# Moving one block product ahead, copies before splits, and two product orders in a two-layer decoder trunk

## The chip, the cores and the metric

The kernel runs on one core of one Trainium2 chip. The metric is device time in microseconds (us); lower is better.

## The reference

Two decoder layers on 512 tokens with 1024 features, all in 32-bit floats. Layer 0 mixes with sliding-window attention and a short convolution, layer 1 with chunked gated linear attention. Each layer then has a gated feed-forward part with a convolution and a per-layer embedding:

```python
for i in range(DEPTH):
    h = _rms_norm(x, mix_norm[i])
    x = x + mixer(h)                       # layer 0: attention and convolution; layer 1: gated linear attention
    x = x + _conv_ffn(_rms_norm(x, ffn_norm[i]), ffn_w_up[i], ffn_conv_w[i], ffn_conv_b[i], ffn_w_down[i])
    x = x + _per_layer_embedding(x, p[i], ple_norm[i], ple_w_gate[i], ple_w_proj[i])

def _conv_ffn(h, w_up, conv_w, conv_b, w_down):
    u = _causal_depthwise_conv(h @ w_up, conv_w) + conv_b
    gate, up = jnp.split(u, 2, axis=-1)
    return (jax.nn.gelu(gate, approximate=False) * up) @ w_down

def _per_layer_embedding(x, p_i, norm, w_gate, w_proj):
    gate = jax.nn.sigmoid(_rms_norm(x, norm) @ w_gate)
    return gate * (p_i @ w_proj)
```

The gate of the linear attention comes from 16 low-rank columns: `log_a = log_sigmoid(g_lr @ w_gate_up + gate_bias) / 16`.

## The kernel before

**Split products.** Every 32-bit operand is cut into a high part (ScalarE, an activation that rounds to `fp32r`) and a low part (VectorE, the operand minus its high part). One product is then three matmuls: high by high, high by low, low by high (`mm3`, L171 to L173). Weights arrive in `raw` (two buffers) by SyncE's DMA queue and are cut by `cut` (L151, L152) or `cut_blocks` (L843, L844) into `wh` and `wl` (three buffers each). Activations are cut by `split` (L109, L110, or L113, L114 with a gain).

**Seven block products.** Some matrix products are taken as 2 x 2 blocks with seven products instead of eight. `seven` (L888) is a generator that issues them on TensorE, 12 matmuls of 256 columns each (L906 to L908). In order: the first goes into bank `W`, and ScalarE copies it into the left halves of `X` and `Y` (L912, L913, by the helper at L900); then it yields. The second goes into `V`, which is copied aside (`so`), the third onto `X` left, the fourth onto `Y` left; `Y` left is copied to `X` right; it yields. Then the last weights are cut, the fifth goes onto `X` right, and `X` right is copied to `Y` right; it yields. The sixth goes onto `Y` left, the seventh onto `X` right, and the last yield gives `X`, `Y` and the copy of `V`. The four forms of the weights are differences of blocks: `first_forms` (L867, L868) and `more_forms` (L875, L878), formed in `raw` by VectorE. `W`, `V`, the projections, transposes and the spread norm share the four PSUM banks of tag `pa`; `X`, `Y` and plain products share the four of tag `ps`.

**Order.** Inside a `manual_schedule` block TensorE runs in the order in which the program is written. The other engines, and TensorE outside such blocks, are put in order by a planner ahead of time: it simulates the kernel with estimated durations and takes, among what is ready on an engine, the one written first; `high_priority` moves work ahead, and `issue_after(ins)` makes what is written in its block come after `ins` on the same engine. A buffer or bank is given out when its first instruction is planned. Each engine then runs its own fixed list.

**Down-projection** (`down`, L1169). A list of plain product parts (`steps`) with block groups between them: four groups in layer 0, three in layer 1. In a group, six matmuls of 512 columns of plain work stand between the block products. `pump` cuts the weights of later parts.

**Layer 0's last stage** (`ple0`, L1368). Four groups of block products for the gate, two feature blocks each; `proj(m)` is the projection of feature block m (six matmuls of 512 columns into a `pa` bank), and `close` applies the norm `R`, the sigmoid (L1417), the projection (L1418) and the residual (L1419). `R` is spread over partitions after group 0 (`spread`, L366, copied by ScalarE at L368). `enter` splits features for layer 1 (L113, L114). Before, per group on TensorE: first product; second to fourth; for groups 1 to 3 a projection; fifth; a projection; sixth and seventh. Group 0's two projections stand ahead of everything.

**Layer 1's mixer** (`mixer1`). `log_decays` turns the low-rank columns (L1735), splits them (L1740 to L1742) and multiplies (L1746), written after the first query product. TensorE is ordered by the planner here. **Layer 1's last stage** (`ple1`, L1457) has its own `proj` over tokens, with `mm3`; its order is written by hand for TensorE, VectorE and ScalarE.

Of the kernel before, what the change touches and what calls it, by code (L numbers as in the profile page):

```python
# [15 lines left out]
ALU = mybir.AluOpType  # L16
# [7 lines left out]
ND = D // P  # L24
# [39 lines left out]
class Kernel:  # L64
# [1104 lines left out]
    def down(self, i, acts, forms, both, work, finish, copied, ahead):  # L1169
# [100 lines left out]
        with tc.manual_schedule(engines={ET.PE}):  # L1270
            with tc.high_priority(offset=300):
                for _ in range(2):
                    load(loads.pop(0))
                with tc.issue_after(copied.ins):
                    pump(0)
            for t, (u, name, k0, k1, s) in enumerate(plan):
                if t in ahead:
                    ahead[t]()
                own = u not in banks
                if own:  # L1280
                    banks[u] = [self.ps(), self.ps()]
                ends = t + 1 == len(plan) or plan[t + 1][0] != u
                joined = i == 0 and u == 3

                def steps(lo, hi):
                    for k in range(lo, hi):
                        for c in range(2):
                            self.mm3(
                                banks[u][c], cuts[t](k, c * P, (c + 1) * P), acts[rows[name][0] + k0 + k],
                                start=own and k == 0, stop=ends and k == k1 - k0 - 1, skip_group_check=joined,  # L1290
                            )

                def settled(ends):
                    nonlocal next_unit
                    if ends:
                        for c in range(2):
                            add(2 * u + c, banks[u][c])
                        due[u] -= 1
                    while not block_left and next_unit < 4 and not due[next_unit]:
                        for m in (2 * next_unit, 2 * next_unit + 1):  # L1300
                            finish(m)
                        next_unit += 1

                if s is None:
                    steps(0, k1 - k0)
                    settled(ends)
                    pump(1)
                    pend()
                    if work:
                        work.pop(0)()  # L1310
                        if not work:
                            load_inner(inner.pop(0))
                else:
                    g = gens[s]
                    steps(0, 1)
                    next(g)
                    steps(1, 2)
                    next(g)
                    steps(2, 3)
                    next(g)  # L1320
                    cut_done(s)
                    pump(1)
                    steps(3, 4)
                    pump(1)
                    settled(ends)
                    X, Y, V = next(g)
                    pump(1)
                    x = self.xT[2 * s + 1].rearrange("p (u t) -> p u t", u=2)
                    nc.vector.tensor_tensor(x, x, V.unsqueeze(1).to_broadcast([P, 2, H]), ALU.add)
# [38 lines left out]
    def ple0(self, fp, both, next_gain):  # L1368
# [17 lines left out]
        def prepare(raw, odd=None, last=None):  # L1386
            ev, od = self.by_parity(raw)
            return self.seven(od, self.seven_forms(ev, od, raw, odd), operands, lambda: result()[:, :H], True, last)

        pT = self.pT  # L1390
        steps = prepare(load(0), self.odd_split, self.last_split)
        wj = self.wj

        def proj(m):
            pj = self.pa()
            c = slice(m * P, (m + 1) * P)
            for k in range(2):
                self.mm3(pj, [w[:, k, c] for w in wj], pT[k], start=k == 0, stop=k == 1)
            return pj

# [21 lines left out]
        late = None  # L1422
        with tc.manual_schedule(engines={ET.PE}):
            pjs = [proj(0), proj(1)]
            for g in range(groups):
                ends = g + 1 == groups
                if not ends:
                    raw = load(g + 1)
                next(steps)
                if late:  # L1430
                    close(*late)
                if ends:
                    enter(0, 1)
                copied = next(steps)
                if ends:
                    enter(2, 3)
                if g:
                    pjs = [proj(2 * g)]
                else:
                    self.end_norm()  # L1440
                    self.begin_norm(None)
                next(steps)
                if g:
                    pjs.append(proj(2 * g + 1))
                last = steps
                if not ends:
                    with nullcontext() if g else tc.issue_after(copied.ins):
                        steps = prepare(raw)
                late = g, next(last), pjs
                if g == 0:  # L1450
                    R = self.spread()
            enter(4, 5)
            close(*late)
            enter(6, 7)
        self.end_norm()

    def ple1(self, fp):  # L1457
# [63 lines left out]

        def proj(t, w):
            pj = self.pa()
            for k in range(2):
                self.mm3(pj, sl(pT[k], t), (w[0][:, k, :], w[1][:, k, :]), start=k == 0, stop=k == 1)
            return pj

        def result():
# [110 lines left out]
    def mixer1(self):  # L1639
# [4 lines left out]
        with tc.tile_pool(name="m1", bufs=1) as mp:  # L1644
# [31 lines left out]
            def pair_w(c0):  # L1676
                return self.weights(w_in[:, :, c0 : c0 + 256], ND, 256)

            def feature(w, c):
                ps = self.ps()  # L1680
                for k in range(ND):
                    self.mm3(ps, w(k, c * P, (c + 1) * P), xg[k], start=k == 0, stop=k == ND - 1)
                return ps

            def query(w, h):
                o = qT[h] = self.fp.tile([P, S], F32, tag="a0", name=self.nm("qT"))
                nc.vector.scalar_tensor_tensor(
                    out=o, in0=feature(w, h % 2), scalar=float(GDK**-0.5), in1=R, op0=ALU.mult, op1=ALU.mult
                )

            def key(w, h):
# [23 lines left out]
            las = []  # L1715

            def gate_up():

# [9 lines left out]
                nc.vector.tensor_tensor(ws[64:96], w[64:96], t[64:96].bitcast(F32), ALU.subtract)  # L1728
                return ws

            def log_decays():

                ps = self.pa()
                for t in range(NT):
                    nc.tensor.transpose(ps[:GR, t * P : (t + 1) * P], glr[:, t, :], self.ident)  # L1735
                gT = self.sp.tile([P, S], F32R, tag="R", name="gT")
                nc.vector.tensor_copy(
                    gT[:96].rearrange("p (a b) -> p a b", b=P), self.ones[:96].unsqueeze(1).to_broadcast([96, NT, P])
                )
                nc.scalar.activation(gT[:GR], ps[:GR], AF.Copy)  # L1740
                nc.scalar.activation(gT[64 : 64 + GR], ps[:GR], AF.Copy)
                nc.vector.tensor_tensor(gT[32 : 32 + GR], ps[:GR], gT[:GR].bitcast(F32), ALU.subtract)  # L1742
                es, pzs = [], []
                for h in range(GH):
                    pz = self.pa()
                    mm(pz, wgs[:96, h * GDK : (h + 1) * GDK], gT[:96], start=True, stop=True)  # L1746
                    e = new()
                    nc.scalar.activation(e, pz, AF.Abs)
                    pzs.append(pz)
                    es.append(e)  # L1750
                for e in es:
                    nc.scalar.activation(e, e, AF.Exp, scale=-1.0)
                for e in es:
                    nc.scalar.activation(e, e, AF.Ln, bias=1.0)
                for h, (e, pz) in enumerate(zip(es, pzs)):
                    la = mp.tile([P, S], F32, tag=f"lah{h}", name=self.nm("la"))
                    nc.vector.scalar_tensor_tensor(
                        out=la, in0=pz, scalar=0.0, in1=e, op0=ALU.min, op1=ALU.subtract
                    )
                    las.append(la)  # L1760
# [346 lines left out]
```

## Time and profile before

| | |
|---|---|
| median of 3 runs | 1200.19 us (1199.80 to 1201.39) |
| the profiled execution | 1199.51 us, its span 1197.5 us |
| granted TensorE clock | 1.00 |
| TensorE matmuls in use | 99% of the span |
| TensorE weight loads | 90% |
| VectorE | 83% |
| ScalarE | 58% |
| GpSimd | 4% |
| HBM traffic | 97 GB/s over the span |

A timeline row is: start in us from the span's start, duration in us, engine, line of the kernel, operation, out<-in, shape, and in brackets the idle time before it and what ended that. PE is TensorE, PEld its weight loads, DVE VectorE, ACT ScalarE, POOL GpSimd. Matmuls are pipelined and the end of one is modelled, so stalls of TensorE are best read from start to start. A row of the waits is: engine and line, what it waited for, total us, how often, the longest. A row of stretches is: stretch, length, then busy us (and instructions) of PE, PEld, DVE, ACT and POOL, the clock, the DMA share and GB/s.

Stages of the span: layer 0's mixer to about 135 us, its feed-forward part to 520, its last stage 521 to 575; layer 1's mixer to about 740, its feed-forward part to 1138, its last stage to the end.

### The profile page before, as it was taken

The page shows a single profiled execution, that of the slowest core. Times are in us where ns is not written, and L with a number is a line of the kernel's source. Part 1 is how long each engine was busy: PE and PEld are TensorE (multiplying, and loading weights), DVE is VectorE, ACT ScalarE, POOL GpSimd, SP SyncE. Part 2 cuts the span into 40 slices and gives each one's busy share as a digit, 9 for nine tenths or more (in the row PEclk, how much of TensorE's full clock was granted, in tenths as well). Part 3 has the DMA queues.
Part 4 walks back from the last instruction along what each step waited for, and adds up shares of the span by engine and source line. Part 5 has one row for each costly group of instructions (what it writes and reads, how often), then busy time and mean ns, then how long its engine had stood idle before and what let it go on. Part 6 is the DMA issues. An engine that isn't in the chain of part 4 may idle for free.

```text
span 1197.5 us, 20218 instructions
## 1 busy us (share of the span) xinstructions
PE 1188.8 (99%) x8218; PEld 1079.3 (90%) x8218; DVE 993.4 (83%) x1593; ACT 690.6 (58%) x1137; POOL 45.2 (4%) x64
## 2 busy tenths in 40 slices
PE   9999999999999999999999999999999999999998
PEld 8877789999999989889978988899999999888887
DVE  6786687898999986899779876687989999978595
ACT  7466565655565653766663655555555556655374
POOL 2610000000000000000100000000000000000000
PEclk9999999999999999999999999999999999999999
DMA  7232222333332342321322222223333333323601
GB/s 223 73 95 81 74 88 71 106 106 106 106 104 91 126 136 86 129 71 61 115 94 71 73 69 71 88 72 111 101 112 101 106 106 115 124 89 97 211 1 71
DMA packets 112928, 117.76 MB, mean 98 GB/s; under 512 B 2840, under 2 KB 107858, under 8 KB 112836
## 3 DMA queue, kind: packets, MB, share of 16 engines
q1 hardware_dynamic: 112000, 115.88, 29.9%
q8 instruction: 64, 1.05, 0.4%
q0 software_dynamic: 560, 0.42, 0.3%
q14 instruction: 28, 0.23, 0.1%
q10 hardware_dynamic: 276, 0.18, 0.1%
HBM read 114.37 MB, written 2.10 MB: 97 GB/s over the span
## 4 chain that ended last, share of the span: by engine, by line
PE 89%; DVE 7%; ACT 2%; issue 1%; DMA 1%; ACTq 0%; POOL 0%; DVEq 0%
PE ps L171 12%; PE ps L172 12%; PE ps L173 12%; PE pa L173 7%; PE pa L172 7%; PE pa L171 7%; PE ps L906 6%; PE ps L908 6%; PE ps L907 5%; PE pa L908 2%; PE pa L906 2%; PE pa L907 2%; PE ps L1505 1%; PE ps L1504 1%; PE ps L1503 1%; DVE wl L152 1%
## 5 line engine op out<-in xcount | busy, mean ns | idle before, releaser
L152 DVE TENSOR_TENSOR wl<-raw,wh 128x1024 fp32r<-128x1024 f32 (+4 forms) x142 | 162.7, 1147 | 41.7 <-ACT wh L151 41.0
L151 ACT ACTIVATE wh<-raw 128x1024 fp32r<-128x1024 f32 (+4 forms) x142 | 141.2, 997 | 83.6 <-PE ps L172 54.0
L843 ACT ACTIVATE wh<-raw 128x1024 fp32r<-128x1024 f32 x90 | 95.6, 1063 | 125.6 <-DVE raw L868 84.2
L961 DVE SCALAR_TENSOR_TENSOR zt<-z,vfa,zt 128x510 f32<-128x510 f32 (+1 forms) x176 | 131.0, 745 | 0.3
L844 DVE TENSOR_TENSOR wl<-raw,wh 128x1024 fp32r<-128x1024 f32 x90 | 110.0, 1222 | 16.5 <-ACT wh L843 15.2
L173 PE MATMUL pa<-b,wl 128*128 128x256 f32 x352 | 97.3, 276 | 0.0
L173 PE MATMUL pa<-a,wl 128*128 128x256 f32 x352 | 97.3, 276 | 0.0
L171 PE MATMUL pa<-b,wh 128*128 128x256 f32 x352 | 97.2, 276 | 0.0
L172 PE MATMUL pa<-b,wh 128*128 128x256 f32 x352 | 97.2, 276 | 0.0
L171 PE MATMUL pa<-a,wh 128*128 128x256 f32 x352 | 97.2, 276 | 0.0
L172 PE MATMUL pa<-a,wh 128*128 128x256 f32 x352 | 97.2, 276 | 0.0
L959 ACT ACTIVATE zt<-z,vfb 128x512 f32<-128x512 f32 x88 | 71.3, 810 | 18.2 <-DVE z L951 9.2
L171 PE MATMUL ps<-b,wh 128*128 128x512 f32 x192 | 76.7, 399 | 0.0
L172 PE MATMUL ps<-b,wh 128*128 128x512 f32 x192 | 75.1, 391 | 0.0
L173 PE MATMUL ps<-b,wl 128*128 128x512 f32 x192 | 75.0, 390 | 0.0
L173 PEld LDWEIGHTS pa<-b,wl 128*128 128x128 f32 x352 | 66.1, 188 | 0.1
L172 PEld LDWEIGHTS pa<-a,wh 128*128 128x128 f32 x352 | 66.1, 188 | 0.0
L172 PEld LDWEIGHTS pa<-b,wh 128*128 128x128 f32 x352 | 66.1, 188 | 0.0
L171 PEld LDWEIGHTS pa<-a,wh 128*128 128x128 f32 x352 | 66.1, 188 | 0.0
L171 PEld LDWEIGHTS pa<-b,wh 128*128 128x128 f32 x352 | 66.1, 188 | 0.0
L173 PEld LDWEIGHTS pa<-a,wl 128*128 128x128 f32 x352 | 66.1, 188 | 0.0
L906 PE MATMUL ps<-four,wh 128*128 128x256 f32 x232 | 64.6, 279 | 0.0
(468 smaller groups left out, 3759.1 us busy)
## 6 DMA issues: line engine op xcount, KB each, us to landing
raw<-in_ffn_w_up_dram SPq DMA_DIRECT2D x42, 1024.0 KB, 4.9
raw<-in_ffn_w_down_dram SPq DMA_DIRECT2D x13, 1024.0 KB, 5.2
raw<-in_hy_w_in_dram SPq DMA_DIRECT2D x8, 1024.0 KB, 5.0
raw<-in_gla_w_in_dram SPq DMA_DIRECT2D x8, 1024.0 KB, 5.1
raw<-in_ffn_w_down_dram SPq DMA_DIRECT2D x8, 768.0 KB, 4.7
raw<-in_ple_w_gate_dram SPq DMA_DIRECT2D x6, 1024.0 KB, 5.2
raw<-in_hy_w_out_dram SPq DMA_DIRECT2D x16, 256.0 KB, 4.2
raw<-in_gla_w_out_dram SPq DMA_DIRECT2D x4, 1024.0 KB, 4.9
```

The source lines that it names most:

```text
L151: nc.scalar.activation(hv, v, AF.Copy)
L152: self.rest_cut = nc.vector.tensor_tensor(lv, v, hv.bitcast(F32), ALU.subtract)
L171: mm(out, lh, rh, start=start, stop=False, **kw)
L172: mm(out, lh, rl, start=False, stop=False, **kw)
L173: mm(out, ll, rh, start=False, stop=stop, **kw)
L843: nc.scalar.activation(h, src, AF.Copy)
L844: nc.vector.tensor_tensor(l, src, h.bitcast(F32), ALU.subtract)
L906: mm(out, wh, xh, start=first and j == 0, stop=False, **kw)
L907: mm(out, wh, xl, start=False, stop=False, **kw)
L908: mm(out, wl, xh, start=False, stop=j == ND // 2 - 1, **kw)
L959: nc.scalar.activation(y, z, AF.Identity, scale=w2[:, f : f + 1], bias=bb[:, f : f + 1])
L961: nc.vector.scalar_tensor_tensor(out=y[:, tap:], in0=z[:, : S - tap], scalar=w[:, f : f + 1], in1=y[:, tap:], op0=ALU.mult, op1=ALU.add,)
```

## The change

- `down`: the first `pump` of a block group comes, on ScalarE, after the group's last copy between banks (`X` right to `Y` right).
- `ple0`: the first product of group g + 1 is issued ahead of group g's sixth and seventh, right after one projection for group g + 1; the other projection stands between the fourth and the fifth product. In the last group that projection is cut into two halves, around the fifth product. `close` of a group comes at the head of the next group; at the end `close` comes ahead of the splits of features 4 and 5. The edge that put group 1's cuts behind group 0's copy is dropped.
- `ple1`: `proj` takes high by high, low by high for both halves of the contraction first, and the weights' low part last.
- `mixer1`: the transposes and splits of the low-rank columns go into the first query product, ahead of its last two contraction steps.

```diff
@@ down
-                    next(g)
+                    copied = next(g)
                     cut_done(s)
-                    pump(1)
+                    with tc.issue_after(copied.ins):
+                        pump(1)
                     steps(3, 4)
                     pump(1)
@@ ple0
-        def proj(m):
-            pj = self.pa()
+        def proj(m, pj=None, ks=(0, 1)):
+            if pj is None:
+                pj = self.pa()
             c = slice(m * P, (m + 1) * P)
-            for k in range(2):
+            for k in ks:
                 self.mm3(pj, [w[:, k, c] for w in wj], pT[k], start=k == 0, stop=k == 1)
             return pj
...
             pjs = [proj(0), proj(1)]
+            next(steps)
             for g in range(groups):
                 ends = g + 1 == groups
                 if not ends:
                     raw = load(g + 1)
-                next(steps)
                 if late:
                     close(*late)
                 if ends:
                     enter(0, 1)
-                copied = next(steps)
+                next(steps)
                 if ends:
                     enter(2, 3)
-                if g:
-                    pjs = [proj(2 * g)]
-                else:
+                if g == 0:
                     self.end_norm()
                     self.begin_norm(None)
+                elif ends:
+                    pjs.append(proj(2 * g + 1, None, (0,)))
+                else:
+                    pjs.append(proj(2 * g + 1))
                 next(steps)
-                if g:
-                    pjs.append(proj(2 * g + 1))
-                last = steps
-                if not ends:
-                    with nullcontext() if g else tc.issue_after(copied.ins):
-                        steps = prepare(raw)
-                late = g, next(last), pjs
+                late = [g, steps, pjs]
+                if ends:
+                    proj(2 * g + 1, pjs[1], (1,))
+                else:
+                    pjs = [proj(2 * g + 2)]
+                    steps = prepare(raw)
+                    next(steps)
+                late[1] = next(late[1])
                 if g == 0:
                     R = self.spread()
-            enter(4, 5)
             close(*late)
-            enter(6, 7)
+            enter(4, 5, 6, 7)
         self.end_norm()
@@ ple1, proj(t, w)
-            for k in range(2):
-                self.mm3(pj, sl(pT[k], t), (w[0][:, k, :], w[1][:, k, :]), start=k == 0, stop=k == 1)
+            for n, (u, v) in enumerate(((0, 0), (1, 0), (0, 1))):
+                for k in range(2):
+                    nc.tensor.matmul(pj, sl(pT[k], t)[u], w[v][:, k, :], start=n + k == 0, stop=n + k == 3)
@@ mixer1
-            def feature(w, c):
+            def feature(w, c, amid=None):
                 ps = self.ps()
                 for k in range(ND):
+                    if amid and k == ND - 2:
+                        amid()
                     self.mm3(ps, w(k, c * P, (c + 1) * P), xg[k], start=k == 0, stop=k == ND - 1)
                 return ps
...
-            def log_decays():
-
+            def turn_low():
                 ps = self.pa()
...
+            def log_decays():
+                gT = low.pop()
...
-            query(w, 0)
+            query(w, 0, turn_low)
             log_decays()
```

More of the change, by code (lines that the diff above doesn't have):

```diff
@@ L1677, in pair_w, with query @@
                 return self.weights(w_in[:, :, c0 : c0 + 256], ND, 256)
-            def feature(w, c):
+            def feature(w, c, amid=None):
                 ps = self.ps()
                 for k in range(ND):
+                    if amid and k == ND - 2:
+                        amid()
                     self.mm3(ps, w(k, c * P, (c + 1) * P), xg[k], start=k == 0, stop=k == ND - 1)
                 return ps
-            def query(w, h):
+            def query(w, h, amid=None):
                 o = qT[h] = self.fp.tile([P, S], F32, tag="a0", name=self.nm("qT"))
                 nc.vector.scalar_tensor_tensor(
-                    out=o, in0=feature(w, h % 2), scalar=float(GDK**-0.5), in1=R, op0=ALU.mult, op1=ALU.mult
+                    out=o, in0=feature(w, h % 2, amid), scalar=float(GDK**-0.5), in1=R, op0=ALU.mult, op1=ALU.mult
                 )
@@ L1714, in mixer1 @@
             new = lambda: mp.tile([P, S], F32, tag="F", name=self.nm("F"), bufs=8)
-            las = []
+            las, low = [], []
             def gate_up():
@@ L1736, in log_decays @@
                 gT = self.sp.tile([P, S], F32R, tag="R", name="gT")
+                low.append(gT)
                 nc.vector.tensor_copy(
```

## The prediction

> **What bounds the kernel now.** I read the page first, then the waits of TensorE, then the timeline around each wait.
>
> ```profile
> span 1197.5 us, 20218 instructions
> PE 1188.8 (99%) x8218; PEld 1079.3 (90%) x8218; DVE 993.4 (83%) x1593; ACT 690.6 (58%) x1137; POOL 45.2 (4%) x64
> ```
>
> TensorE (PE) is in use for 99% of the span. No edit takes a matmul away, so all that can be won is time in which PE stands still. The waits of PE, over the whole run and (third line) from 1040 us to the end, say where ScalarE's copies between banks hold it (total, count, longest):
>
> ```profile
> PE ps L906 <- ACT ps L900: 1.4, 3, 0.6
> PEld ps L906 <- ACT ps L900: 5.0, 12, 0.8
> PEld ps L906 <- ACT ps L900: 1.1, 3, 0.4
> ```
>
> PE shows a wait only beyond the modelled end of its previous matmul, and the weight load counts from its own last load; so I measure a stall from start to start in the timeline. One of the layer 0 down-projection's block groups:
>
> ```profile
> 463.82 1.06 ACT L151 ACTIVATE wh<-raw 128x1024 fp32r<-128x1024 f32 x1 [2.35 <-PE ps L907]
> 464.61 0.39 PE L172 MATMUL ps<-ul,wh 128*128 128x512 f32 x1
> 464.79 0.36 ACT L900 COPY ps<-ps 128x256 f32<-128x256 f32 x1
> 464.84 0.39 PE L173 MATMUL ps<-uh,wl 128*128 128x512 f32 x1
> 464.92 1.23 DVE L152 TENSOR_TENSOR wl<-raw,wh 128x1024 fp32r<-128x1024 f32 x1 [2.91 <-ACT wh L151]
> 465.21 0.39 PE L906 MATMUL ps<-a,wh 128*128 128x256 f32 x1
> 465.43 0.28 PE L907 MATMUL ps<-a,wh 128*128 128x256 f32 x1
> 465.55 0.28 PE L908 MATMUL ps<-a,wl 128*128 128x256 f32 x1
> ...
> 449.12 0.39 PE L173 MATMUL ps<-uh,wl 128*128 128x512 f32 x1
> 449.75 0.39 PE L906 MATMUL ps<-a,wh 128*128 128x256 f32 x1 [0.25 <-ACT ps L900]
> ```
>
> A 512-wide matmul is followed after 0.23 us (464.61 to 464.84), a 256-wide one after 0.12 (465.43 to 465.55). PE should have gone on at 465.07; it started at 465.21, and its second matmul came 0.22 instead of 0.12 later. So a stall has a lost time and a restart of 0.10: here 0.24 us. The cause stands above it: ScalarE was free at 463.82 and took a split of 1.06 us (L151) that nobody needed yet, and the copy started after it.
>
> **The change part by part.** *The copy ahead of the split in the down-projections.* The edge makes the split wait for the copy on ScalarE. Then the copy can start near 463.9, and PE goes on at 465.07. The group shown is layer 0's second and gains 0.24; its first gains 449.75 - 449.12 - 0.23 + 0.10 = 0.50; its third is taken as the second, and its fourth waits nowhere. Layer 1's three waits add up to 1.1 us and are taken at 0.2 each. Together 0.24 + 0.50 + 0.24 + 0.6 = **-1.6 us** (bounds 0 and -1.8). What it costs: the split comes some 0.4 us later, so its low half on VectorE ends near 466.55 instead of 464.92 + 1.23 = 466.15. It is used after the two products that begin at 465.07 (24 x 0.12 = 2.9 us), at 468. That covers it by 1.4 us, so zero.
>
> *The first product of the next group, put ahead of the last two of this one (layer 0's last stage).* Two stalls lie at the seams of groups 0 and 1:
>
> ```profile
> 532.07 0.28 PE L908 MATMUL ps<-b,wl 128*128 128x256 f32 x1
> 532.44 0.36 ACT L900 COPY ps<-ps 128x256 f32<-128x256 f32 x1 [0.80 <-PE ps L908]
> 532.85 0.39 PE L906 MATMUL ps<-a,wh 128*128 128x256 f32 x1 [0.50 <-ACT ps L900]
> 535.69 0.60 PE L366 MATMUL pa<-cf,rtok 128*128 128x128 f32 x4
> 536.04 0.36 PE L906 MATMUL pa<-a,wh 128*128 128x256 f32 x1
> 536.32 0.59 ACT L368 COPY R<-pa 128x512 f32<-128x512 f32 x1 [0.52 <-PE pa L366]
> 538.78 0.28 PE L908 MATMUL pa<-b,wl 128*128 128x256 f32 x1
> 539.28 0.63 ACT L900 COPY ps<-pa 128x256 f32<-128x256 f32 x2
> 539.69 0.38 PE L906 MATMUL ps<-a,wh 128*128 128x256 f32 x1 [0.64 <-ACT ps L900]
> ```
>
> At 532.85 group 0's sixth product waits for the copy of the fifth, with no work between: 532.85 - 532.07 - 0.12 + 0.10 = 0.76. After the change a projection (6 x 0.23 = 1.4 us) and the next group's first product (12 x 0.12 = 1.4) stand there. At 539.69 group 1 waits for the copies of its first product: 539.69 - 538.78 - 0.12 + 0.10 = 0.89; after the change two products more lie between. Both go: **-1.65 us**.
>
> It adds a wait as well. `pa` has four banks. When R is spread, they hold the projections 0, 1 and now 2, and the next first product, whose bank R takes once it is copied out. Group 1's second product then finds no bank until ScalarE has copied R. Today the first product stands behind the spread (536.04) and covers that copy; moved, it doesn't. The copy ends at 536.32 + 0.59 = 536.91; PE follows a copy 0.05 later (532.44 + 0.36 = 532.80, start 532.85), so it stands 536.96 - 536.04 = **+0.92 us**. It can't be less without another bank; one split in front of the copy (1.07, below) would make it 2.0.
>
> The earlier first product needs its weights earlier:
>
> ```profile
> 530.29 0.36 ACT L900 COPY ps<-ps 128x256 f32<-128x256 f32 x1
> 530.56 1.07 ACT L843 ACTIVATE wh<-raw 128x1024 fp32r<-128x1024 f32 x1
> 532.03 1.22 DVE L844 TENSOR_TENSOR wl<-raw,wh 128x1024 fp32r<-128x1024 f32 x1
> ```
>
> Their low half is ready at 533.25. The third matmul, which reads it first, would come at 532.19 + 1.4 + 2 x 0.23 = 534.0 or, with 256-wide ones, 533.8: covered by 0.5 us, zero. These rows also show the copy at 530.29 ahead of the split at 530.56: the edge that ordered them is dropped. Whether the order stays is the planner's choice; zero in the sum, priced as a rival.
>
> In the last group one projection is cut in halves and covers two copies with 0.69 us each, where 1.4 stood. The copies there, and the last matmuls before them:
>
> ```profile
> 567.42 0.28 PE L908 MATMUL ps<-b,t 128*128 128x256 f32 x1
> 568.42 0.37 ACT L900 COPY ps<-ps 128x256 f32<-128x256 f32 x1
> 570.25 0.28 PE L908 MATMUL ps<-b,wl 128*128 128x256 f32 x1
> 571.71 0.37 ACT L900 COPY ps<-ps 128x256 f32<-128x256 f32 x1
> ```
>
> If they run as late as here, PE waits until 568.84 instead of 567.42 + 0.12 + 0.69 = 568.23, and until 572.13 instead of 571.06: 0.61 + 1.07 + 2 x 0.10 = 1.9 us. If they start as promptly as at 532.44 (0.37 after the last matmul's start), 0.37 + 0.36 + 0.05 = 0.78 fits into 0.12 + 0.69: zero. I take a third, **+0.6**, since the copies have priority among ready work and matmuls of the next stage can fill a gap that the planner foresees.
>
> At its end, `close` now stands ahead of the splits of features 4 and 5:
>
> ```profile
> 575.89 0.68 DVE L1411 TENSOR_TENSOR zt<-ps,R 128x512 f32<-128x512 f32 x1
> 576.63 0.43 PE L171 MATMUL ps<-wh,b 128*128 128x368 f32 x1 [0.28 <-DVE zt L1411]
> ```
>
> The next layer's third bank waits for that read. Between the 0.28 shown and that with restart and pipelining (about 0.5): **-0.4** (0 to -0.5).
>
> *The two product orders and the early transposes.* In layer 1's start the transposes of the low-rank gate move into the query's matmuls. In its last stage the projection's low half is used last:
>
> ```profile
> 600.54 0.39 PE L172 MATMUL ps<-b,wh 128*128 128x512 f32 x1
> 601.39 0.50 PE L1746 MATMUL pa<-gT,wgs 96*128 96x512 f32 x1 [0.46 <-DVE gT L1742]
> ...
> 1156.47 1.22 DVE L1483 TENSOR_TENSOR wl<-four,wh 128x1024 fp32r<-128x1024 f32 x1
> 1156.74 0.39 PE L171 MATMUL pa<-wh,four 128*128 128x512 f32 x1
> 1157.74 0.50 PE L172 MATMUL pa<-wl,four 128*128 128x512 f32 x1 [0.61 <-DVE wl L1483]
> ```
>
> The first stall is 601.39 - 600.54 - 0.23 + 0.10 = 0.72. Six matmuls (1.4 us) come between now, but this stage's order is the planner's, and it misjudged the wait once: **-0.5** (0 to -0.7). The second is 1157.74 - 1156.74 - 0.23 + 0.10 = 0.87. The low half is needed at the fifth matmul, 1156.74 + 4 x 0.23 = 1157.66, and comes at 1157.74: **-0.75**.
>
> The new order changes the stationary operand six times a product instead of four.
>
> ```profile
> L172 PEld LDWEIGHTS pa<-wl,four x4: 186/187/188, 1157.7 to 1159.7; 128*128 128x128 f32 x4
> ```
>
> L172 keeps L171's stationary operand and loads it again in 187 ns; the page has as many loads as matmuls. At 464.61 to 464.84 the load is one of a changed operand and is hidden. So nothing is added. The Trainium skill ("TensorE: Matmul & The Clock Gate", "The mechanism") says that weight loads overlap running matmuls only where the row group differs. By it a change of operand would be exposed; loads and matmuls here add up to more than the span, so the trace doesn't agree.
>
> Sum: -1.6 - 1.65 + 0.92 + 0.6 - 0.4 - 0.5 - 0.75 = **-3.4 us**. The profiled execution took 1199.51 us (2.0 more than its span), 0.7 below the median of 1200.19, so 1196.1 there and 1196.8 against the median. A measurement of this kernel can tell about 0.2% (2.4 us) from no change.
>
> **The rivals.** *A, copies late on ScalarE (0.17).* The dropped edge lets the split of 530.56 go first (the copy 1.0 late, +1.0), R's copy falls behind a split (+1.07), the last group pays 1.9 (+1.3): 3.4 us, all that was won: 1200.2. For it: the copies at 568.42 and 571.71 came 0.6 and 1.1 later than promptly. Against it: ScalarE is 58% busy.
>
> *B, slower: the low half of the early product's weights is late (0.10).* From 562 to 575 us VectorE has no room:
>
> ```profile
> 562.00:575.00 13.00, 13.00 (x100) 12.18 (x99) 12.99 (x20) 10.30 (x19) 0.00 (x0) 1.00 0.19 59
> ```
>
> (busy PE, loads, VectorE 12.99, ScalarE.) PE works in order: a first product that waits now also holds up the two ready products behind it. It happens three times. It decides from 3.4 / 3 = 1.1 us a group, one low half of 1.22. Two in front of it give 3 x 2.44 - 3.4 = +3.9: 1204.1. Against it: the 0.5 us in hand at group 0, the tightest seam by my reading.
>
> *C, the change doesn't do what it says (0.06).* The planner puts other work ahead of the copies, whatever the edge: the 1.6 is missing, 1198.4, not to be told from the same.
>
> *D, exposed loads (0.01).* Two more changed operands in each of eight products at 187 ns: +3.0, so 1199.8.
>
> **How the numbers follow.** The forecast has 0.66; its own range is 1194.6 (new waits in the last group zero, all gains full) to 1197.8. Faster 0.68 (forecast and a part of C), same 0.21 (A, most of C, D), slower 0.11 (B and the worst of A). The range takes in A and leaves out B: 1194.6 to 1200.5.
>
> **What would show it.** Right: no start-to-start gap over 0.15 before L906 in either down-projection; none at groups 0 and 1's two seams; one new wait of about 0.9 us before group 1's second product, for ScalarE's L368; L1746 and L172 in the last stage without waits. Wrong: PE waits for DVE L844 ahead of a first product (B), a split on ScalarE ahead of a copy in group 0 or 3 (A), or new waits in layer 1's mixer that none of these steps names.

## The result: slower by 0.3%, and the profile after

The median is 1204.66 us (1202.48 to 1205.64) against 1200.19; the ratio is 1.0031, with a 95% interval of 1.002 to 1.0043, given below in square brackets behind each ratio. The forecast was 1196.8. The profiled execution took 1203.26 us, its span 3.7 us more than before. The page after shows its engines and the head of its chain (which gave PE 89% and DVE 7% before):

```profile
span 1201.2 us, 20215 instructions
PE 1188.5 (99%) x8218; PEld 1079.6 (90%) x8218; DVE 993.6 (83%) x1593; ACT 691.0 (58%) x1137; POOL 46.7 (4%) x64
PE 84%; DVE 11%; ACT 3%; issue 1%; DMA 1%; ACTq 0%; DVEq 0%
```

The work of each engine is nearly that of before (VectorE 993.6 against 993.4 us, ScalarE 691.0 against 690.6); PE stands still longer, and mostly for VectorE. The waits of PE after, over the whole run (what it waited for; total, count, longest), without one of 1.3 us at the start of the span that both kernels have:

```profile
PE ps L172 <- DVE wl L152: 2.3, 1, 2.3
PE pa L906 <- ACT R L368: 1.6, 1, 1.6
PE ps L906 <- ACT ps L900: 1.3, 3, 0.7
...
PE ps L171 <- DVE xT L1263: 0.9, 2, 0.6
PE pa L908 <- DVE wl L844: 0.3, 2, 0.2
```

The first was named in no step. It stands in layer 1's first product, the Values of the linear attention (L171 to L173 with 368 columns), whose weights are cut in four parts of two contraction steps each. The first two low halves before:

```profile
572.90 1.75 DVE L152 TENSOR_TENSOR wl<-raw,wh 128x736 fp32r<-128x736 f32 x2
```

After, the second part's high half on ScalarE, then VectorE, then PE:

```profile
573.27 0.82 ACT L151 ACTIVATE wh<-raw 128x736 fp32r<-128x736 f32 x1 [0.47 <-PE ps L907]
574.98 0.92 DVE L152 TENSOR_TENSOR wl<-raw,wh 128x736 fp32r<-128x736 f32 x1
...
577.49 0.69 DVE L1413 TENSOR_TENSOR zt<-ps,R 128x512 f32<-128x512 f32 x1 [0.39 <-PE ps L908]
...
583.16 0.92 DVE L152 TENSOR_TENSOR wl<-raw,wh 128x736 fp32r<-128x736 f32 x1
580.98 0.83 PE L171 MATMUL ps<-wh,b 128*128 128x368 f32 x4
584.13 0.43 PE L172 MATMUL ps<-wl,b 128*128 128x368 f32 x1 [2.32 <-DVE wl L152]
```

PE waits for the second part: eight matmuls of L172 (two contraction steps in four banks) stand ahead of the one that waits. Before, VectorE cut the second low half right behind the first, at 573.73, ahead of the last group's `close` (whose L1411 starts at 575.89). After, its high half is there at 573.27 + 0.82 = 574.09, but VectorE takes the operations of `close`, L1413 to L1421, first, with 0.39 us of standstill among them, and cuts the low half only at 583.16, 9.4 us later than before. The last of the four matmuls at 580.98 began at 580.98 + 3 x 0.17 = 581.48; the next should have begun at 581.65 and began at 584.13: 2.48 us, and 0.10 of restart.

The three other costs of the stage come from copies behind splits on ScalarE and from shorter covers in the last group:

```profile
529.65 2.00 ACT L843 ACTIVATE wh<-raw 128x1024 fp32r<-128x1024 f32 x2
531.56 0.37 ACT L900 COPY ps<-ps 128x256 f32<-128x256 f32 x1
531.98 0.39 PE L906 MATMUL ps<-a,wh 128*128 128x256 f32 x1 [0.70 <-ACT ps L900]
539.53 1.06 ACT L843 ACTIVATE wh<-raw 128x1024 fp32r<-128x1024 f32 x1 [0.63 <-DVE raw L878]
540.49 0.57 ACT L368 COPY R<-pa 128x512 f32<-128x512 f32 x1
541.11 0.38 PE L906 MATMUL pa<-a,wh 128*128 128x256 f32 x1 [1.57 <-ACT R L368]
571.67 0.39 PE L906 MATMUL ps<-a,wh 128*128 128x256 f32 x1 [0.41 <-ACT ps L900]
574.42 0.39 PE L906 MATMUL ps<-a,wh 128*128 128x256 f32 x1 [0.20 <-ACT ps L900]
```

Start to start with restart they lose 0.97 (without the edge, two splits went ahead of the copy), 1.84 (R's copy behind one split), and 0.69 + 0.48 (the halved projection). The stall that stood at 539.69 before, the second seam, is gone, as forecast.

In the down-projections the edge did what it says, and the time went elsewhere:

```profile
464.13 0.36 ACT L900 COPY ps<-ps 128x256 f32<-128x256 f32 x1 [2.46 <-PE ps L908]
464.40 1.06 ACT L151 ACTIVATE wh<-raw 128x1024 fp32r<-128x1024 f32 x1
465.26 0.28 PE L906 MATMUL ps<-a,wh 128*128 128x256 f32 x1
...
452.67 0.68 DVE L1263 TENSOR_TENSOR xT<-xT,ps 128x512 f32<-128x512 f32 x1
453.40 0.50 PE L171 MATMUL ps<-uh,wh 128*128 128x512 f32 x1 [0.61 <-DVE xT L1263]
472.72 0.39 PE L908 MATMUL pa<-a,wl 128*128 128x256 f32 x1 [0.17 <-DVE wl L844]
```

The copy is ahead of the split and PE goes from L173 to L906 without a gap. But the split, here 0.58 us later, pushes VectorE's list back: PE loses 0.88 us to an addition that frees a bank (L1263) and 0.45 to the next group's low half (L844). The fourth group's copy, which nobody waited for before, now costs 0.24 at 496.13. Layer 1 repeats the first two (0.59 and 0.45).

The next table adds up, over all matmuls that follow one with a 128 by 128 stationary operand, how much later each starts than its predecessor's usual spacing (the median of its width before: 0.227 us for 512 columns, 0.113 for 256 and so on). Only excesses over 0.085 us count. By stretches of the span:

| us of the span | before | after |
|---|---|---|
| 0 to 440 | 5.84 | 5.58 |
| 440 to 520, layer 0's down-projection | 1.10 | 1.66 |
| 520 to 606, its last stage and layer 1's first products | 4.02 | 7.77 |
| 606 to 740, layer 1's mixer | 13.40 | 13.00 |
| 740 to 1120, feed-forward | 1.50 | 2.18 |
| 1120 to the end | 1.33 | 0.55 |
| sum | 27.2 | 30.7 |

The difference, 3.5 us, is nearly the span's 3.7. Of the 0.68 of the feed-forward row, 0.15 lies in layer 1's down-projection (from 1050 us on); the rest lies ahead of it, where the kernels do not differ, and so shows how far single profiles scatter. The median lost 0.8 us more than the span (1204.66 - 1200.19 = 4.47): four of seven runs lie at 1204.7 to 1205.6, three at 1202.5 to 1203.3. What sets them apart is under e11.

### The profile page after: what moved, and what is told of

Read it like the earlier page. It is cut to its first block, busy times and chain, and to the rows that moved or that the text cites. A ratio compares the mean times of both kernels' runs of the same rounds, so it can differ in the third digit from the quotient of the medians.

```text
span 1201.2 us, 20215 instructions
## 1 busy us (share of the span) xinstructions
PE 1188.5 (99%) x8218; PEld 1079.6 (90%) x8218; DVE 993.6 (83%) x1593; ACT 691.0 (58%) x1137; POOL 46.7 (4%) x64
## 4 chain that ended last, share of the span: by engine, by line
PE 84%; DVE 11%; ACT 3%; issue 1%; DMA 1%; ACTq 0%; DVEq 0%
PE ps L171 11%; PE ps L172 11%; PE ps L173 11%; PE pa L172 6%; PE pa L173 6%; PE pa L171 6%; PE ps L906 5%; PE ps L907 5%; PE ps L908 5%; PE pa L908 2%; PE pa L906 2%; PE pa L907 2%; DVE wl L844 2%; PE ps L1509 1%; PE ps L1508 1%
## 5 line engine op out<-in xcount | busy, mean ns | idle before, releaser
L844 DVE TENSOR_TENSOR wl<-raw,wh 128x1024 fp32r<-128x1024 f32 x90 | 109.9, 1221 | 17.6 <-ACT wh L843 17.5
L173 PE MATMUL pa<-b,wl 128*128 128x256 f32 x352 | 97.3, 276 | 0.1
L173 PE MATMUL pa<-a,wl 128*128 128x256 f32 x352 | 97.2, 276 | 0.0
L171 PE MATMUL pa<-a,wh 128*128 128x256 f32 x352 | 97.2, 276 | 0.0
L171 PE MATMUL pa<-b,wh 128*128 128x256 f32 x352 | 97.2, 276 | 0.0
L172 PE MATMUL pa<-a,wh 128*128 128x256 f32 x352 | 97.2, 276 | 0.0
L172 PE MATMUL pa<-b,wh 128*128 128x256 f32 x352 | 97.2, 276 | 0.0
L171 PE MATMUL ps<-b,wh 128*128 128x512 f32 x192 | 76.6, 399 | 0.0
L172 PE MATMUL ps<-b,wh 128*128 128x512 f32 x192 | 75.1, 391 | 0.0
L173 PE MATMUL ps<-b,wl 128*128 128x512 f32 x192 | 75.0, 391 | 0.0
L173 PEld LDWEIGHTS pa<-b,wl 128*128 128x128 f32 x352 | 66.1, 188 | 0.3 <-DVE wl L152 0.3
L171 PEld LDWEIGHTS pa<-b,wh 128*128 128x128 f32 x352 | 66.1, 188 | 0.0
L172 PEld LDWEIGHTS pa<-a,wh 128*128 128x128 f32 x352 | 66.1, 188 | 0.0
L172 PEld LDWEIGHTS pa<-b,wh 128*128 128x128 f32 x352 | 66.1, 188 | 0.0
L171 PEld LDWEIGHTS pa<-a,wh 128*128 128x128 f32 x352 | 66.1, 188 | 0.0
L173 PEld LDWEIGHTS pa<-a,wl 128*128 128x128 f32 x352 | 66.1, 188 | 0.0
L906 PE MATMUL ps<-four,wh 128*128 128x256 f32 x232 | 64.7, 279 | 0.0
```

The costliest lines, as they stand in the source:

```text
L171: mm(out, lh, rh, start=start, stop=False, **kw)
L172: mm(out, lh, rl, start=False, stop=False, **kw)
L173: mm(out, ll, rh, start=False, stop=stop, **kw)
L844: nc.vector.tensor_tensor(l, src, h.bitcast(F32), ALU.subtract)
L906: mm(out, wh, xh, start=first and j == 0, stop=False, **kw)
```

## Experiments

**Each part alone.** The kernel before with one part of the diff.

e1: `ple0` alone.


> The kernel before with the reordering of layer 0's last stage alone. Theory 1 (the stage itself loses: a copy behind a split in group 0, the wait for R, the two half covers, and the low half of the next layer's weights late behind close): about +3.5 us. Theory 2 (the loss comes from the edges in the down-projections, and the stage gains what was forecast): -1 us.


Measured 1202.73 us (1202.02 to 1205.52), 1.0027 [1.0018, 1.0037], with the waits of the full change (2.48, 1.71, 0.87, 0.56 and 0.37 us without restarts). Most of the loss is here: theory 1.

e2: the down-projections' edge alone.


> The kernel before with the edge in the two down-projections alone. Theory 1: the copy waits (about 1.6 us in both layers) go, but the split that now comes 0.3 to 0.5 us later delays VectorE's list, so that a bank is freed late in the first group and the low half of the next group's weights comes late in the second: +0.5 to +1.0 us in all. Theory 2 (the forecast): -1.6 us.


1200.70 us (1200.04 to 1201.74), 1.0009 [1.0000, 1.0018]: a small loss in place of -1.6, theory 1.

e3: layer 1's product order alone.


> The kernel before with the new product order in layer 1's last stage alone. Both theories: -0.7 us. If weight loads of a changed operand were exposed, +3 us.


1199.18 us (1198.27 to 1200.13), 0.9996 [0.9987, 1.0005]. The medians differ by -0.64, and the interval takes in no change; the trace is clearer: the stall at the low half fell from 0.88 to 0.20 us (0.089 and a restart). Six changes of the stationary operand a product cost nothing that can be seen.

e4: the early transposes alone.


> The kernel before with the low-rank transposes in the midst of the first query product alone. Both theories: -0.5 us, the wait before L1746's place gone; 0 if the planner only moves the wait.


1199.69 us (1198.88 to 1200.43), 0.9997 [0.9988, 1.0006]; the medians differ by -0.13, and the interval takes in no change. The wait for gT fell only from 0.62 to 0.44, and a new one for ScalarE's Values copies (0.42 with restart) came: nearer to the second expectation.

The four differences of the medians (+2.91, +0.88, -0.64, -0.13) add up to +3.0 us, 1.5 less than the whole change lost.

**One rearrangement of `ple0` at a time put back.** Each starts from e1 (1202.73).

e5: the splits of features 4 and 5 ahead of `close`.

```
+            enter(4, 5)
             close(*late)
-            enter(4, 5, 6, 7)
+            enter(6, 7)
```

> The part in layer 0's last stage alone (1202.73 us on its own), with one thing put back: the splits of features 4 and 5 again come ahead of close at the stage's end. Theory 1, the order on VectorE: close's ten vector operations leave no gap in front of the low half of the Values' weights, and PE waits 2.48 us for it at L172. With the old order that wait goes and a wait of up to 0.5 us for the third bank comes back: 1200.2 to 1200.7. Theory 2, the low half is late because the whole stage ends closer together and VectorE is behind by itself: the wait stays, 1202.7.


1206.39 us (1204.07 to 1207.03), 1.0048 [1.0036, 1.0061]: a miss for both. The 2.48 us wait is gone, and the low half that it was for runs at 578.45, amid `close`: so the order is its cause. But ScalarE's list was planned anew as well. Waits of PE:

```profile
PE ps L171 <- ACT wh L151: 1.8, 2, 1.6
...
PE pa L1739 <- ACT glr L1675: 1.1, 1, 1.1
```

At 594 to 598 us layer 1's query waits for its split and the transposes of the gate's low-rank columns for their copy: 3.1 us in the place of 2.6.

e6: the edge between group 0's copy and group 1's preparation.

```
-                next(steps)
+                copied = next(steps)
...
-                    steps = prepare(raw)
+                    with nullcontext() if g else tc.issue_after(copied.ins):
+                        steps = prepare(raw)
```

> The part in layer 0's last stage alone (1202.73 us), with the dropped edge put back: group 1's preparation is issued behind the copy between group 0's fifth and sixth product. Theory 1, the split that goes first on ScalarE is the whole of the 0.97 us wait at the sixth product: it goes, 1201.8; and since the next splits move, R's copy may come ahead of the split that stands in front of it now, which takes up to 0.9 of the 1.82 there: down to 1200.9. Theory 2, the split then comes late and the early first product waits for its low half instead: no gain, 1202.7.


1201.86 us (1201.29 to 1202.45), 1.0013 [1.0004, 1.0022]. The 0.97 is gone and R's wait fell to 1.47; the Values' wait fell too, to 1.4, and the last group's copies rose by 0.4. Theory 1 in kind, with shifts elsewhere that it does not give.

e7: projection 2 in group 1.

```
+                    if g == 1:
+                        pjs = [proj(2)]
                     pjs.append(proj(2 * g + 1))
...
-                    pjs = [proj(2 * g + 2)]
+                    if g:
+                        pjs = [proj(2 * g + 2)]
```

> The part in layer 0's last stage alone (1202.73 us), with projection 2 computed in group 1 and not in group 0, so that one bank more is free when R is spread. Theory 1, the 1.82 us wait before group 1's second product is for the bank that R's copy holds: it goes, 1200.9, and the 0.97 at group 0's sixth product stays. Theory 2, the second product would have waited for its operands or weights then anyway: most of the 1.82 comes back under another name, 1202 to 1202.7.


1209.23 us (1208.02 to 1209.36), 1.0072 [1.0058, 1.0086]. R's bank is waited for no longer, which shows the cause; but another plan came with it:

```profile
PE pa L348 <- DVE acc L294: 5.8, 1, 5.8
```

The sum for layer 1's norm (L348) stands in PE's fixed order behind the first four of the Values' matmuls, and VectorE adds up its squares late.

e8: only the first products moved; projections, edge and end as before the change. The edit holds those of e5 and e6; of the rest, the part on the projections:

```
-                elif ends:
-                    pjs.append(proj(2 * g + 1, None, (0,)))
-                else:
-                    pjs.append(proj(2 * g + 1))
+                else:
+                    pjs = [proj(2 * g)]
                 next(steps)
+                if g:
+                    pjs.append(proj(2 * g + 1))
...
```

> The kernel before with only the first product of the next group moved amid the preceding group: projections, the edge in group 0 and the order at the end stand as before. Theory 1 (the loss comes from the three other rearrangements, each by a wait of its own): the waits of 0.97, 1.82, 1.17 and 2.59 us are all gone, and so are the two seams of 0.76 and 0.89 us of the kernel before: 1199.8 - 1.65 = 1198.2. Theory 2 (moving the product itself makes VectorE and ScalarE late): 1199.8 or more.


1204.89 us (1204.18 to 1207.33), 1.0043 [1.003, 1.0055]. None of the four named waits is left. In their place come the query's wait as in e5 (1.13 + 1.61 us), the norm's sum (1.04), and three first products that wait for their low half (0.90, 0.49, 0.49), rival B's mechanism: theory 2.

e9: only group 1's first product moved, into group 0.

```
+                if g != 1:
                     next(steps)
...
+                    if g == 0:
+                        next(steps)
```

> The kernel before with one product moved, group 1's first, put ahead of the last two of group 0; all other groups, the projections, the edge and the stage's end stand as before. Theory 1 (the seams can be won where nothing else is moved): the 0.76 and 0.89 us at the two seams go, at most one split ahead of R's copy comes back where nobody waits for R's bank: 1199.8 - 1.65 = 1198.2. Theory 2 (ScalarE and VectorE are ordered by a plan made over the whole stage, and any move reorders the entry into layer 1): 1199.8 or more, with a wait for the low half of the Values' weights or for ScalarE's copies at 575 to 600 us.


1201.30 us (1200.60 to 1202.19), 1.0007 [0.9998, 1.0016]. Theory 2. Waits of PE:

```profile
PE pa L1738 <- ACT glr L1674: 1.5, 1, 1.5
...
PE pa L908 <- DVE wl L844: 0.8, 1, 0.8
```

The low half of the moved product ends at 532.94 and PE waits 0.93 us for it. The forecast had 0.5 us in hand, with a projection (1.4 us) in front; here none stands there. So of the 1.65 us that both seams lost before, 0.93 is paid again here, and the gate's transposes cost 1.6 more at 593.4.

e10: the down-projections' part (e2), its additions with priority.

```
         def add(m, ps):
-            nc.vector.tensor_tensor(self.xT[m], self.xT[m], ps, ALU.add)
+            with tc.high_priority(offset=60):
+                nc.vector.tensor_tensor(self.xT[m], self.xT[m], ps, ALU.add)
```

> The down-projections' part alone (1200.70 us), with the additions that free the banks given priority on VectorE. Theory 1, the gain of the copies (1.0 us in layer 0) is lost because the split that now stands behind the copy pushes VectorE's list back, and the addition that frees a bank comes late (0.87 us at 453.95): that wait goes, and about as much in layer 1 (0.59): 1199.3 to 1199.8. Theory 2, the bank would be free in time and PE waits for its operands: nothing is won, 1200.7.


1203.79 us (1202.80 to 1204.70), 1.0029 [1.0018, 1.0041]: a miss. No wait for L1263 is left, so that was its cause; but the additions now push the splits back, and PE waits for those:

```profile
456.80 0.39 PE L906 MATMUL pa<-a,wh 128*128 128x256 f32 x1 [0.16 <-ACT wh L843]
458.06 0.39 PE L908 MATMUL pa<-a,wl 128*128 128x256 f32 x1 [0.76 <-DVE wl L844]
```

e2 had one such wait in each layer, e10 has three in layer 0 (0.92, 0.46, 0.53 us). From 450 to 455 us VectorE is busy 4.86 of 5.00 us, so there the order decides which of the two comes late.

**The largest wait in the changed kernel itself.**

e11: the changed kernel with

```
-            v = Values(672, 1040, 352)
+            with tc.high_priority(offset=60):
+                v = Values(672, 1040, 352)
```

The lists of ScalarE and VectorE ahead of 575 us stay as they are.


> The changed kernel (1204.66 us, from 1202.5 to 1205.6) with one thing more: the splits of the first Values' weights get priority over close. Theory 1, the wait of 2.59 us for their low half at 584 us costs its own length and, in about half of the runs, a halved TensorE clock for some microseconds behind it: without it the time falls by 2.6 in the fast runs and the upper group of runs is gone: median 1200.5 to 1201, spread about 1.5 us as before the change. Theory 2, the scatter has nothing to do with that wait: the median falls by 2.6 to 1202.0 and the runs still spread over 3 us.


1200.79 us (1200.25 to 1202.02), 1.0006 [0.9998, 1.0015] against before, 3.9 below the changed kernel. Waits of PE from 520 to 610 us:

```profile
PE pa L906 <- ACT R L368: 1.6, 1, 1.6
PE ps L906 <- ACT ps L900: 1.3, 3, 0.7
PE pa L907 <- DVE b L110: 0.2, 1, 0.2
```

The low half runs at 576.25, ahead of `close`. The wait is gone and nothing in this stretch took its place, and the upper group of runs is gone too: theory 1. This is the one clean removal of the study. It won 3.9 us, 1.3 more than the wait's 2.58. What such a wait can cost besides shows in e8, whose profiled run (1206.66 us) is one of its two longest. By stretches (PE, loads, VectorE, ScalarE, GpSimd busy, then PE's granted clock):

```profile
590.00:594.00 4.00, 4.00 (x27) 3.69 (x25) 0.00 (x0) 2.00 (x6) 0.00 (x0) 1.00 0.31 106
594.00:597.00 3.00, 0.59 (x3) 0.17 (x2) 1.11 (x2) 2.97 (x6) 0.00 (x0) 0.91 0.00 0
597.00:603.00 6.00, 5.69 (x13) 4.28 (x14) 4.27 (x4) 3.29 (x5) 0.00 (x0) 0.50 0.35 100
603.00:609.00 6.00, 6.00 (x27) 4.87 (x27) 1.92 (x2) 2.86 (x5) 0.00 (x0) 0.98 0.21 75
```

PE does almost nothing from 594 to 597, and then runs at half its clock for 6 us: 13 matmuls where 27 go in the next 6. e5 has the same two waits, 1.13 and 1.61 us, with a clock of 1.00 throughout in its profiled run of 1204.07, its fastest; its four others lie at 1206.3 to 1207.0. So the same waits trip the clock in some runs and not in others. That the upper runs of the changed kernel had this too is inferred: none of them was profiled. Besides e11, the mean clock on record for each run speaks for it: 0.998 or 0.999 in three of the four upper runs, 1.000 in the three lower ones; in e1, 0.998 in its two longest runs (1204.41, 1205.52) and 1.000 in the seven others. The fourth upper run (1204.66) has 1.000 and stays unexplained.

e12: e6 with e11's priority.


> The part in layer 0's last stage alone with the edge in group 0 put back (1201.86 us) and the splits of the first Values' weights given priority. Left of the waits are R's bank (1.47 us), the last group's two copies (1.5) and whatever the new order brings; gone are the edge's 0.97 and the Values' wait (1.4). Theory 1 (waits add up): 1201.86 - 1.4 = 1200.4. Theory 2 (priority there starves close and the norm of the next layer): a new wait takes the gain, 1201.5 or more.


1206.33 us (1205.59 to 1206.53), 1.0051 [1.0037, 1.0065]. Theory 2: the Values' wait is gone, and the gate's transposes (2.5 us) and the query's split (1.6 us) wait at 591 to 598, with the half clock behind them. The same edit that won 3.9 us in e11, on the whole change, lost 4.5 here, on e6.

**Can the moved product win anything?**

f1: e9 with the product order and the early transposes.


> The kernel before with group 1's first product moved into group 0 (alone: 1201.30 us) and, beside it, the change's two parts outside this stage: the early transposes and the product order of layer 1's last stage. Theory 1, the 1.96 us that the moved product alone lost at 593.4 us, where the low-rank gate's transposes wait for ScalarE, is paid only because these transposes stand right there; moved into the query's matmuls they wait for nothing: 1201.3 - 1.96 - 0.64 - 0.2 = 1198.5. Theory 2, ScalarE is late there for all its work: the query's own product waits in their place and only the product order's gain is left, 1200.6.


1200.26 us (1199.16 to 1201.29), 0.9999 [0.9990, 1.0008], near theory 2. The transposes, traced amid the query's matmuls, still stand in front of them on PE, and wait:

```profile
PE pa L1740 <- ACT glr L1675: 1.7, 1, 1.7
```

This stage's order is the planner's: where the program calls the transposes doesn't fix where they run.

f2: the changed kernel without the down-projections' edge, with e6's edge and e11's priority.


> The changed kernel without the down-projections' edges, with group 0's edge put back and priority for the splits of the first Values' weights. Theory 1, waits add up once the early transposes are there: 1200.8 (with the Values' splits first) - 0.9 (down-projections) - 1.0 to 1.4 (edge, R's copy) = 1198.5 to 1198.9. Theory 2, the edge and the priority together make ScalarE late at the entry into layer 1, as without the early transposes (1206.3): 1201 or more.


1205.66 us (1204.72 to 1206.49), 1.0042 [1.0028, 1.0056]. Theory 2, by e12's waits. So the early transposes and the product order, which e12 lacks, do not help; beside e11, f2 has the edge in group 0 more and the down-projections' edge less.

f3: f2 with e7's later projection 2.


> As the run with both put back, and projection 2 again in group 1, so that R's copy holds no bank that is waited for. Theory 1, the 1.4 us for R's bank go: 1197.1 to 1197.5. Theory 2, the stage's plan is made anew and the norm or the Values' weights of layer 1 come late, as when this was done alone (1209.2, a wait of 6.0 us): 1200 or more.


1198.11 us (1196.96 to 1199.42), 0.9978 [0.9969, 0.9987]: faster than both kernels, and nearest theory 1, though 0.6 us above it. Its span is 1195.4. Its waits from 520 to 610 us:

```profile
PE ps L906 <- ACT ps L900: 0.8, 1, 0.8
PE pa L908 <- DVE wl L844: 0.7, 1, 0.7
```

These are 0.99 us at the last group's first copy and 0.88 for the moved product's low half. Counted as in the table, the stretch from 520 to 570 has 2.93 us against 2.55 before: the stage with the moved product won nothing. The gain is behind it: 570 to 606 has 0.18 against 1.47, the last stage 0.64 against 1.33. Another 0.93 lies ahead of 440 us, where the kernels do not differ, so not all that the span won, 2.1, is f3's. e7's edit, which alone lost 6.5 us, here gained 7.55: no such edit has a price of its own.

f4: the product order and the early transposes alone.


> The kernel before with the change's two parts that won by themselves: layer 1's last stage's product order (-0.64) and the early transposes (-0.13). If they add up 1199.4; if the early transposes' new wait (0.42 us for ScalarE's Values copies) grows, 1199.8.


1199.31 us (1198.39 to 1201.06), 0.9988 [0.9979, 0.9996]. The early transposes' new wait for the Values copies is 0.70 us with restart here. Against that batch's median of before, 1200.54, it is -1.2, with an interval of -2.5 to -0.5 that takes in the -0.8 of the two parts alone.

## Why the prediction was wrong, step by step

- **Copies ahead of splits (-1.6).** The three copies' waits in layer 0 went as worked out. The part that failed is "covered by 1.4 us, so zero": it followed the delayed split to its own matmul and not to what stands behind it on VectorE, an addition that frees a bank and the next group's low half. By the table it came to +0.56 in layer 0, not -1.0, and to +0.15 in layer 1, not -0.6.
- **The two seams (-1.65).** Half right. The second went (0.89). At the first, the dropped edge let two splits go first, rival A's first mishap: 0.97 in the place of 0.76. Where the edge was kept and no projection stood in front (e8, e9, f3), the low half was late instead: 0.88 to 0.93, rival B's mechanism.
- **R's bank (+0.92).** Mechanism right (e7 takes it away), size 1.84: the split in front, for which 2.0 had been given.
- **The last group (+0.6).** 1.17, inside the bounds; the planner put one of the Values' matmuls ahead of each copy's reader.
- **`close` moved ahead (-0.4).** The step that failed most. The wait at 576.63 went (-0.55). But the range was 0 to -0.5, which excluded a loss, and the step did not ask which work `close` gets ahead of on VectorE: the second low half of layer 1's first weights, cut at 573.73 before and at 583.16 after, behind all of `close`. It cost 2.58 us in the profile, and 3.9 in the median by e11; that the clock makes up the difference is inferred.
- **Early transposes (-0.5)** came to -0.5 inside the change and to -0.13 alone. **Product order (-0.75)**: -0.69 in the profile, -0.64 alone. Rival D is out.

After, for these two (the transposes and the query behind them, then L1530's products):

```profile
600.80 0.60 PE L1741 MATMUL pa<-cf,glr 128*16 128x128 f32 x4
601.15 0.48 PE L171 MATMUL ps<-b,wh 128*128 128x512 f32 x1
...
1161.09 1.07 PE L1530 MATMUL pa<-wh,four 128*128 128x512 f32 x4
1162.08 0.73 PE L1530 MATMUL pa<-wl,four 128*128 128x512 f32 x2
```

The lower end of the range, 1194.6, is reached only without R's 0.92, of which the prediction says that it can't be less; with it, all gains in full (1.8, 1.65, 0.5, 0.7, 0.87) give about 1195.6. Rival A gave 1200.2 and rival B 1204.1. That B's number lies near the measured 1204.66 is luck: in the changed kernel no first product of layer 0's last stage waits for its low half. What happened was both of A's copies, and B's engine, VectorE full from 562 us on, at a place that B did not look at. The list of what would show it wrong did name that place: new waits in layer 1's mixer. Behind the single terms stands a wrong assumption: that an edit changes only the waits beside it. ScalarE and VectorE are ordered by a plan, and e5, e7, e8, e12 and f2 each removed the waits that they aimed at and lost more at the entry into layer 1. By what rule the plan chooses there is not settled; f3's good order was found, not worked out.

## What to carry to other kernels

Before an operation is moved on a full engine, list what it is moved past up to the next stage's first weights; a step whose range excludes a loss needs that list. Where a planner orders the engines, price an edit by the whole order that it makes, and try to pin the few operations that the next stage's first matmuls read (it won in e11; in e12 and f2 the same pin was not enough). A copy that goes first on ScalarE delays a split, and with it VectorE's list: follow the delay to every reader behind it, not only to the split's own.

## What the runs showed of the hardware

A wait of TensorE of 2 to 3 us can cost as much again: in e8, 6.0 us of work at half the clock cost about 3.0. Read in half-microsecond stretches, e8's clock fell to one half at 596.46 us, 2.2 us after its burst of matmuls and transposes ended at 594.31 (one transpose between), and came back at 603.29, 6.0 us after PE was busy again. e7's (a 6.0 us wait):

```profile
576.00:582.00 6.00, 0.25 (x2) 0.14 (x2) 6.00 (x11) 3.27 (x6) 1.95 (x5) 0.69 0.00 0
582.00:588.00 6.00, 5.62 (x19) 5.22 (x20) 3.69 (x7) 0.00 (x0) 2.13 (x2) 0.50 0.32 94
588.00:594.00 6.00, 6.00 (x37) 6.00 (x35) 2.20 (x3) 2.17 (x4) 0.00 (x0) 0.96 0.72 229
```

It fell at 578.22, 2.1 us into the wait, and rose at 588.46, 6.6 us after its end. The half clock lasted 3.41 us in e12 (from 597.63 on), 6.83 in e8 and 10.24 in e7, once, twice and three times the same length. The Trainium skill ("TensorE: Matmul & The Clock Gate", "Part 1: The HAM clock gate") says that the clock is halved after an idle window of about 3.4 us, that the window runs free of the program, and that the point of transition therefore varies from run to run. The lengths and the scatter agree; that a whole window must be idle does not, since 2.1 us in e7, right behind matmuls, were enough.
